# One core, two transformer blocks in float32: paired products counted once by the planner, a compression in quarters of the array, and 512-column tails and memory values

## The chip, the cores and the metric

The kernel runs on one core of one Trainium2 chip. The metric is the device time of one execution in microseconds (us); lower is better. The kernel before takes 2112.3 us, the median of three runs (2111.91 to 2114.06). The profiled execution took 2107.61 us, of which the span from the first to the last instruction is 2105.8 us.

## The reference

Two blocks, each of two layers, on 256 tokens of width 1024, all in float32.

- Block 1, per layer: `mixer1` (a gated linear recurrence, a forgetting attention with 8 heads that the kernel calls `fox`, a retention with 4 heads called `ret`), a cross attention to a memory of 256 rows (4 heads of 256), and a feed-forward part (`silu(h @ w_gate) * (h @ w_up)) @ w_down`, hidden width 2816).
- Block 2, per layer: a feed-forward part, `mixer2`, and a second feed-forward part. `mixer2` joins three attentions: a sparse one called `nsa` (8 heads), a stick-breaking one called `sb` (4 heads) and a window attention called `swa` (4 heads).

Of `nsa` one piece matters here, the compression of keys and of values:

```python
def compress(t, w1, w2):
    blocks = t[:, cmp_idx] + cmp_pos[:, None, :]        # 15 windows of 32 tokens, stride 16
    blocks = blocks.transpose(0, 3, 1, 2, 4).reshape(B, G, n_cmp, CMP_LEN * Dh)   # 2 * 15 rows of 2048
    return jax.nn.silu(blocks @ w1) @ w2                # w1: 2048 x 256, w2: 256 x 64
```

and of the cross attention the memory's keys and values, `mem_n @ w_k` and `mem_n @ w_v`, which depend on no earlier layer.

## The kernel before

**Weights.** Every weight passes through one class (`Weights`, from line 155). `plan` lists the chunks in the order of use. A chunk of at most 2048 columns (1 MB) is loaded by SP into one of three `raw` buffers. It is cut into pieces of 1024 columns, and each piece is split into a rounded part and a rest: ACT makes `whi` (the value cast to fp32r), DVE makes `wlo` (the raw value minus `whi`). Six pieces may be made ahead. A raw buffer comes free when its last piece is split, and then the next chunk is loaded. The activations are split in the same way (`thi`, `tlo`; `ahi`, `alo` in the feed-forward part; `mhi`, `mlo` for the memory), and a product is three matmuls: hi by hi, hi by lo, lo by hi (`mm3`). Small products of the attentions are plain float32; the profile shows each of those as two matmul records.

**Main and side work.** The products by the large weights are the main work, written in program order. Everything else (softmax, transposes, norms) is side work: Python generators in a list. After each half piece, `pump` (line 336) asks which generator's next step is due and writes it there. Due times come from `Pace` (line 49), a small model of the engines that is kept while the program is written: `nc.products` is when TensorE would be through with what is written so far, `nc.end` when a side step's results would be there. A step is written once its inputs are due by at most 0.3 us after `nc.products`. Where the main work needs a result that no step has delivered yet (`need`), `pump(force=True)` writes the remaining steps without main work between them. This document calls such a stretch forced.

**Pairs.** Two heads are worked on side by side: the first in the lower 64 rows or columns of the TensorE array, the second in the upper ones (`pair_scores`, `pair_scores_T`, `pair_pv`). `Pace` adds up the time of both.

**Feed-forward (`ffn`, planned at line 773).** The hidden width 2816 is five blocks of 512 columns and a tail of 256. For each block the gate products are made, ACT applies silu, the up products are made, DVE multiplies. The tail is two blocks of 256 columns, gate and up, each with its own accumulator of the two that rotate.

**Memory keys and values.** They are 16 units that fill gaps between other work (`fill_steps`, line 1170), each for 256 output columns: 48 matmuls of 256 columns, an ACT copy to `kvout` (one buffer) and a DMA to DRAM.

**Compression.** `compress_blocks` (line 1625) writes the windows, and `put` splits them on ACT and DVE. `compress_mm` (line 1647) then makes, for keys and values, 16 steps of `mm3` with 30 stationary and 256 moving columns: 96 matmuls in a layer, in eight pieces that stand between pieces of the gate weights. `compress_attention` (line 1727) transposes the result, and only there are the second weights `w2` and some small constants loaded, by SP, behind the large chunks in its queue. The output of `compress_attention` (`pcT`) is needed by the fourth and the eighth unit of `nsa`.

## Time and profile before

| what | value |
|---|---|
| median of three runs | 2112.3 us |
| profiled execution: its time, its span | 2107.61 us, 2105.8 us |
| mean granted TensorE clock | 0.995 of full speed |
| busy share: TensorE (PE), weight load, DVE, ACT, POOL | 97%, 82%, 61%, 53%, 4% |
| HBM read, mean rate | 372 MB, 180 GB/s |

Busy time of PE counts each matmul with its way through the array, so neighbours overlap. What a matmul adds to the time is the distance from its start to the next one's start, which the view in order of time shows. All lines read L150 because one helper records every instruction; groups are told apart by the names of the tiles.

### The profile page before, as it was taken

To read this page: it belongs to the slowest core of one execution; us is meant where nothing else is said; L and a number is where in the kernel's file an instruction comes from. 1 tells how busy PE (TensorE), PEld (TensorE's weight loads), DVE (VectorE), ACT (ScalarE), POOL (GpSimd) and SP (SyncE) were. 2 spreads that over 40 slices of the span, in tenths; PEclk is the share of its full clock that TensorE was granted. 3 is DMA by queue.
4 is the path that set the end of the run, shared out by engine and by line. 5 is a ranking of instruction groups with operands and counts; after the bars stand their busy time and mean duration, and the time that the engine had idled before them with its cause. 6 is when DMAs were issued, how large, how long until landed. Compare 5 with 4: busy or idle time off the path is not lost.

```text
span 2105.8 us, 28507 instructions
## 1 busy us (share of the span) xinstructions
PE 2053.1 (97%) x10982; PEld 1717.3 (82%) x10982; DVE 1276.0 (61%) x2187; ACT 1120.7 (53%) x1910; POOL 84.7 (4%) x110
## 2 busy tenths in 40 slices
PE   7999999999899999999999999999999999999999
PEld 6889888888797788788888767888888887768887
DVE  6766566556664755655467666664655567756553
ACT  5556566455465654555355655554555456446552
POOL 0210000002100000000001000000000001000000
PEclk9999999999999999999999999999999999999999
DMA  7555565654465565555646544555555547545553
GB/s 244 182 194 190 186 212 180 212 178 158 148 225 175 182 198 191 172 187 180 210 145 207 169 140 158 193 176 193 180 196 194 162 151 230 144 132 183 179 197 103
DMA packets 204583, 380.86 MB, mean 181 GB/s; under 512 B 14160, under 2 KB 78464, under 8 KB 204448
## 3 DMA queue, kind: packets, MB, share of 16 engines
q1 hardware_dynamic: 192928, 366.46, 53.1%
q10 hardware_dynamic: 11520, 12.59, 2.0%
q8 instruction: 86, 1.41, 0.3%
q14 instruction: 49, 0.40, 0.1%
HBM read 372.03 MB, written 6.99 MB: 180 GB/s over the span
## 4 chain that ended last, share of the span: by engine, by line
PE 83%; DVE 6%; ACT 4%; DMA 4%; issue 2%; POOL 0%; SPq 0%; ACTq 0%; DVEq 0%; POOLq 0%
PE acc L150 74%; PE aux L150 6%; DVE wlo L150 3%; PE o L150 3%; ACT whi L150 1%; DMA nb<-cdram 1%; DMA raw<-in_w_in_dram 1%; DMA w<-in_nsa_cmp_k_w_dram 1%; ACT rn L150 1%; ACT thi L150 1%; DMA kvd<-kvout 0%; SPq L150 0%; DVE t L150 0%; DVE h L150 0%; DMA mem<-in_mem_dram 0%
## 5 line engine op out<-in xcount | busy, mean ns | idle before, releaser
L150 PE MATMUL acc<-whi,thi 128*128 128x512 f32 (+2 forms) x1856 | 716.2, 386 | 2.3 <-ACT thi L150 1.4
L150 PE MATMUL acc<-whi,tlo 128*128 128x512 f32 (+2 forms) x1856 | 699.9, 377 | 2.5 <-DVE tlo L150 2.4
L150 PE MATMUL acc<-wlo,thi 128*128 128x512 f32 (+2 forms) x1856 | 699.3, 377 | 3.1 <-DVE wlo L150 2.8
L150 DVE TENSOR_TENSOR wlo<-raw,whi 128x1024 fp32r<-128x1024 f32 (+1 forms) x386 | 463.0, 1210 | 310.1 <-ACT whi L150 308.3
L150 ACT CAST whi<-raw 128x1024 fp32r<-128x1024 f32 (+1 forms) x386 | 393.7, 1037 | 243.9 <-PE acc L150 219.9
L150 DVE SCALAR_TENSOR_TENSOR wlo<-raw,prm,whi 128x512 fp32r<-128x512 f32 (+1 forms) x640 | 398.5, 680 | 173.8 <-ACT whi L150 173.6
L150 ACT ACTIVATE whi<-raw,prm 128x512 fp32r<-128x512 f32 (+1 forms) x640 | 379.9, 663 | 90.2 <-PE acc L150 86.7
L150 PEld LDWEIGHTS acc<-whi,thi 128*128 128x128 f32 x1856 | 350.3, 189 | 72.4 <-issue 9.3
L150 PEld LDWEIGHTS acc<-whi,tlo 128*128 128x128 f32 x1856 | 349.9, 189 | 70.3 <-DVE tlo L150 6.4
L150 PEld LDWEIGHTS acc<-wlo,thi 128*128 128x128 f32 x1856 | 350.5, 189 | 64.4 <-DVE wlo L150 6.1
L150 PE MATMUL acc<-whi,ahi 128*128 128x512 f32 x528 | 206.9, 392 | 0.0
L150 PE MATMUL acc<-whi,alo 128*128 128x512 f32 x528 | 205.7, 389 | 0.0
L150 PE MATMUL acc<-wlo,ahi 128*128 128x512 f32 x528 | 205.6, 389 | 0.0
L150 PEld LDWEIGHTS acc<-whi,alo 128*128 128x128 f32 x528 | 99.1, 188 | 20.8
L150 PEld LDWEIGHTS acc<-whi,ahi 128*128 128x128 f32 x528 | 99.2, 188 | 19.9
L150 PEld LDWEIGHTS acc<-wlo,ahi 128*128 128x128 f32 x528 | 99.2, 188 | 19.9
L150 POOL TENSOR_TENSOR r<-v,mhalf 128x1 f32<-128x1 f32 (+3 forms) x46 | 48.1, 1047 | 1593.9 <-DVE v L150 1591.9
L150 PE MATMUL acc<-thi,whi 128*128 128x256 f32 x384 | 111.9, 291 | 0.0
L150 PE MATMUL acc<-tlo,whi 128*128 128x256 f32 x384 | 108.6, 283 | 0.0
L150 PE MATMUL acc<-thi,wlo 128*128 128x256 f32 x384 | 108.5, 283 | 0.0
L150 DVE SCALAR_TENSOR_TENSOR silu<-acc,r,silu 128x512 f32<-128x512 f32 (+1 forms) x72 | 47.5, 702 | 100.4 <-PE acc L150 100.4
L150 ACT CAST ahi<-aux 128x512 fp32r<-128x512 f32 (+1 forms) x72 | 39.8, 553 | 121.9 <-PE aux L150 121.7
(301 smaller groups left out, 1946.9 us busy)
## 6 DMA issues: line engine op xcount, KB each, us to landing
raw<-in_w_in_dram SPq DMA_DIRECT2D x65, 1024.0 KB, 5.1
raw<-in_ffn_w_gate_dram SPq DMA_DIRECT2D x44, 1024.0 KB, 5.1
raw<-in_ffn_w_up_dram SPq DMA_DIRECT2D x44, 1024.0 KB, 5.1
raw<-in_ffn_w_down_dram SPq DMA_DIRECT2D x44, 1024.0 KB, 4.9
raw<-in_w_gate_dram SPq DMA_DIRECT2D x22, 1024.0 KB, 5.0
raw<-in_w_up_dram SPq DMA_DIRECT2D x22, 1024.0 KB, 5.1
raw<-in_w_down_dram SPq DMA_DIRECT2D x22, 1024.0 KB, 4.8
raw<-in_w_out_dram SPq DMA_DIRECT2D x16, 1024.0 KB, 5.0
```

What stands on the lines that cost most here:

```text
L150: return f(*args, **kwargs)
```

## The change

- `Pace` counts a product that runs beside another one at 7 ns in place of its columns. The second of each pair in `pair_scores`, `pair_scores_T` and `pair_pv` is marked so.
- Feed-forward tail: gate and up stand side by side in one 512-column block, loaded by two DMAs into one chunk. Silu and multiplication both follow the end of that block.
- Memory values: one accumulator for 512 columns, 48 matmuls of 512 for two units; one copy and one DMA for both. `kvout` is twice as large.
- Compression: `w1` is not split (`split=False`): the raw buffer itself is the moving operand, so it comes free only after the matmuls. The windows are not split either; they are padded to 32 columns with zeros. Four products at a time go to four column quarters of the array, in plain float32, and each quarter holds a part of the sum. A product by four stacked unit matrices (`sel`) adds the parts and transposes.
- The second weights and the constants are loaded when `compress_blocks` starts (`load_small`).
- `swa` waits for `blocks` where it waited for `blocks_ready`; `xs` in `mixer1` has one buffer in place of two.

```diff
-            self.products = start + max(0.027, size(moving) * rate / 2400.0) + 0.004
+            self.products = start + (0.007 if self.beside else max(0.027, size(moving) * rate / 2400.0) + 0.004)
...
-                mm(pss[u][:, c], q[HALF[u], qs], k[HALF[u], ks], start=True, stop=True)
+                mm(pss[u][:, c], q[HALF[u], qs], k[HALF[u], ks], True, True, beside=u > 0)
...
-            for w in (g, u):
-                W.plan(w, c0, c1, 0, 8, 4 if c1 - c0 == 512 else 8, 2 if c1 - c0 == 512 else 4, gain=gain)
+            if c1 - c0 == 512:
+                for w in (g, u):
+                    W.plan(w, c0, c1, 0, 8, 4, 2, gain=gain)
+            else:
+                W.plan(g, c0, c1, 0, 8, 4, 2, gain=gain, beside=u)
...
+                    if n < 512:
+                        hold["n"] = n
+                        gate_done(a)
...
-                    xs = mp.tile([P, 16, 32], F32, tag="xs", name=nm("xs"))
+                    xs = mp.tile([P, 16, 32], F32, tag="xs", name=nm("xs"), bufs=1)
...
+            W.plan(I["w_cv"][l], c // 2 * 512, c // 2 * 512 + 512, 4 * (c % 2), 4 * (c % 2) + 4, 4, 2)
...
+                            mm3(a[:, b * 512 : b * 512 + 512], MT.hi[:, kt, bs], MT.lo[:, kt, bs], hi[:, j, :], lo[:, j, :], kt == 0, kt == 7)
...
-                W.plan(I[f"nsa_cmp_{kv}_w1_2"][l], 0, 256, 8 * k, 8 * k + 8, 8, 4)
+                W.plan(I[f"nsa_cmp_{kv}_w1_2"][l], 0, 256, 8 * k, 8 * k + 8, 8, 4, split=False)
...
-                while "wqk_ready" not in hold or "blocks_ready" not in hold:
+                while "wqk_ready" not in hold or "blocks" not in hold:
...
-                            mm3(a[:30, k * S : k * S + S], bh[:, k, kt, :], bl[:, k, kt, :], hi[:, j, :], lo[:, j, :], kt == 0, kt == 15)
+                            mm(a[32 * j : 32 * j + 32, k * S : k * S + S], blocks[:, k, kt, :], w[:, j, :], i == 0, i == 3, beside=j > 0)
...
-                        turn(ps[:, (2 * k + b) * 30 : (2 * k + b + 1) * 30], raw[:, k * S + b * P : k * S + (b + 1) * P], ident[:30, :30])
+                        mm(ps[:, (2 * k + b) * 30 : (2 * k + b + 1) * 30], raw[:, k * S + b * P : k * S + (b + 1) * P], sel[:, :30], start=True, stop=True)
```

In numbers of matmuls: of the 256-column kind with `whi,thi` (and as many each with `wlo,thi` and `whi,tlo`) 224 become 32, while the 512-column kind goes from 1600 to 1696. For the memory values 128 of each of three kinds become 64 of 512 columns. The 192 compression matmuls become 64.

The first place is TensorE at the first piece of the compression in the first layer of `mixer2` (`o` is the accumulator of the compression, `t` the windows, `acc` the gate products ahead of it). Before, the last main product and the first 6 of 24 rows:

```order
L150 MATMUL acc_10173<-whi_10108,tlo_9112 128x512
L150 MATMUL o_10220<-whi_10126,t_796_10169 30x256
L150 MATMUL o_10220<-wlo_10127,t_796_10169 30x256
L150 MATMUL o_10220<-whi_10126,t_797_10170 30x256
L150 MATMUL o_10220<-whi_10126,t_796_10169 30x256
L150 MATMUL o_10220<-wlo_10127,t_796_10169 30x256
L150 MATMUL o_10220<-whi_10126,t_797_10170 30x256
```

Now, the whole of it:

```order
L151 MATMUL acc_9780<-wlo_9718,thi_8714 128x512
L151 MATMUL acc_9780<-whi_9717,tlo_8715 128x512
L151 MATMUL o_9818<-raw_9590,t_787_9645 32x256 x8
L151 MATMUL acc_9780<-whi_9771,thi_8714 128x512
L151 MATMUL acc_9780<-wlo_9772,thi_8714 128x512
```

Where 24 products stood, 8 stand, and they read the raw buffer.

The second place is TensorE at the end of the first layer of `mixer2`, where the main work needs all of `nsa` (`kT,qT` are a unit's scores, `ident,rn` its transposes, `rn,vsw` its products by the values, `bc,kk` the compressed part, `acc` the main work). Before, the last rows up to the forced stretch, and its first rows:

```order
L150 MATMUL aux_11302<-kT_9547,qT_9546 128x256
L150 MATMUL acc_11167<-whi_11121,thi_9111 128x512
...
L150 MATMUL acc_11333<-whi_11194,tlo_9542 128x512
L150 MATMUL o_11262<-rn_11287,vsw_9545 64x256
L150 MATMUL o_11262<-rn_11289,vsw_9545 64x256
L150 MATMUL o_11262<-rn_11287,vsw_9545 64x128
L150 MATMUL o_11262<-rn_11289,vsw_9545 64x128
L150 MATMUL aux_11357<-ident_90,rn_11309 128x128 x3
L150 MATMUL aux_11358<-ident_90,rn_11314 128x128 x3
```

Now, at the same scores:

```order
L151 MATMUL acc_10772<-whi_10652,tlo_9145 128x512
L151 MATMUL aux_10790<-kT_9150,qT_9149 128x128
L151 MATMUL aux_10791<-kT_9150,qT_9149 128x128
L151 MATMUL aux_10790<-kT_9150,qT_9149 128x256
L151 MATMUL aux_10791<-kT_9150,qT_9149 128x256
L151 MATMUL o_10814<-rn_10766,vsw_9148 64x256
L151 MATMUL o_10814<-rn_10768,vsw_9148 64x256
L151 MATMUL o_10814<-rn_10766,vsw_9148 64x128
L151 MATMUL o_10814<-rn_10768,vsw_9148 64x128
L151 MATMUL aux_10819<-ident_90,rn_10798 128x128 x3
L151 MATMUL aux_10820<-ident_90,rn_10803 128x128 x3
```

The forced stretch began at the values of the sixth unit; now it begins at those of the fifth, and four units' products by the values stand in it where three stood.

The third place is SP's queue around the compression weights of the first layer of `mixer2` (`w20` and `w21` are the second weights; the semaphores in brackets are the engines or queues waited for). Before:

```order
L150 DMA raw182_10195<-in_nsa_cmp_v_w1_2_dram 128x8x256 [waits DMAHW7_49,DVE_49]
L150 DMA raw183_10237<-in_w_in_2_dram 128x4x512 [waits DMAHW0_49,DVE_49]
L150 DMA raw184_10277<-in_nsa_cmp_v_w1_2_dram 128x8x256 [waits DMAHW1_49,DVE_49]
L150 DMA raw185_10315<-in_w_in_2_dram 128x4x512 [waits DMAHW2_49,DVE_49]
...
L150 DMA raw190_10609<-in_w_up_swa_2_dram 64x2x1024 [waits DMAHW5_49,DVE_49]
L150 DMA raw190_10609<-in_w_up_swa_2_dram 64x2x1024
L150 DMA w20_856_10666<-in_nsa_cmp_k_w2_2_dram 128x2x64 [waits DMAHW6_49]
L150 DMA w21_857_10667<-in_nsa_cmp_v_w2_2_dram 128x2x64 [waits DMAHW7_49]
```

Now:

```order
L151 DMA raw178_9590<-in_nsa_cmp_k_w1_2_dram 128x8x256 [waits DMAHW5_49,DMAHW0_49,DVE_49]
L151 DMA w20_781_9633<-in_nsa_cmp_k_w2_2_dram 128x2x64
L151 DMA w21_782_9634<-in_nsa_cmp_v_w2_2_dram 128x2x64
...
L151 DMA raw182_9833<-in_nsa_cmp_v_w1_2_dram 128x8x256 [waits DMAHW2_49,PE_49]
L151 DMA raw183_9855<-in_w_in_2_dram 128x4x512 [waits DMAHW3_49,DMAHW1_49,DVE_49]
L151 DMA raw184_9899<-in_nsa_cmp_v_w1_2_dram 128x8x256 [waits DMAHW4_49,DMAHW0_49,PE_49]
L151 DMA raw185_9955<-in_w_in_2_dram 128x4x512 [waits DMAHW3_49,DMAHW2_49,PE_49]
```

The small weights moved ahead of twelve large chunks, and chunks 182, 184 and 185 wait for TensorE where they waited for DVE.

## Rows read from the trace of the kernel before

**Rows 1.** The page, busy time and share of the span of TensorE.

```profile
PE 2053.1 (97%) x10982; PEld 1717.3 (82%) x10982; DVE 1276.0 (61%) x2187; ACT 1120.7 (53%) x1910; POOL 84.7 (4%) x110
```

**Rows 2.** The page, the chain that ended last, share of the span by engine.

```profile
PE 83%; DVE 6%; ACT 4%; DMA 4%; issue 2%; POOL 0%; SPq 0%; ACTq 0%; DVEq 0%; POOLq 0%
```

**Rows 3.** In order of time: start, duration, matmul, in a feed-forward part and its tail.

```profile
1399.64 0.39 PE L150 MATMUL acc<-whi,thi 128*128 128x512 f32 x1
...
1405.08 0.39 PE L150 MATMUL acc<-whi,thi 128*128 128x512 f32 x1
...
1419.08 0.28 PE L150 MATMUL acc<-whi,thi 128*128 128x256 f32 x1
...
1421.96 0.28 PE L150 MATMUL acc<-whi,thi 128*128 128x256 f32 x1
```

**Rows 4.** Groups by form: count, busy time, mean ns, idle before.

```profile
L150 PE MATMUL acc<-whi,thi 128*128 128x256 f32 x224 | 64.5, 288 | 0.0
L150 PE MATMUL acc<-mhi,whi 128*128 128x256 f32 x128 | 37.9, 296 | 0.0
L150 PE MATMUL o<-whi,t 128*30 128x256 f32 x128 | 24.1, 280 | 1.3 <-DVE t L150 1.3
```

**Rows 5.** In order of time, 24 compression matmuls, first and last.

```profile
1164.32 0.28 PE L150 MATMUL o<-whi,t 128*30 128x256 f32 x1
...
1166.99 0.28 PE L150 MATMUL o<-whi,t 128*30 128x256 f32 x1
```

**Rows 6.** In order of time, a pair of heads by the values, eight records.

```profile
1209.40 0.39 PE L150 MATMUL acc<-whi,tlo 128*128 128x512 f32 x1
1209.72 0.87 PE L150 MATMUL o<-rn,vsw 128*64 128x256 f32 x8
1210.52 0.50 PE L150 MATMUL acc<-whi,thi 128*128 128x512 f32 x1
1210.87 0.40 PE L150 MATMUL acc<-wlo,thi 128*128 128x512 f32 x1
```

**Rows 7.** Chain in order of time: start, duration; four plain float32 products, cross attention.

```profile
200.09 1.73 PE o L150 x8
```

**Rows 8.** Waits of TensorE in the whole run: total us, times, longest.

```profile
PE aux L150 <- DMA w<-in_nsa_cmp_k_w_dram: 3.8, 2, 2.6
PE aux L150 <- DVE rs L150: 2.9, 2, 1.5
...
PE o L150 <- DVE rvg L150: 2.2, 1, 2.2
...
PE acc L150 <- ACT kvout L150: 1.9, 1, 1.9
PE aux L150 <- DVE rot L150: 1.7, 2, 1.5
```

**Rows 9.** In order of time, the forced stretch in `mixer2`, first layer.

```profile
1253.94 0.87 PE L150 MATMUL o<-rn,vsw 128*64 128x256 f32 x8
...
1261.35 1.44 PE L150 MATMUL aux<-ident,rn 128*128 128x128 f32 x6 [2.06 <-DVE rn L150]
1262.73 2.24 PE L150 MATMUL o<-rn,vsw 128*64 128x256 f32 x8
1264.89 1.27 PE L150 MATMUL o<-bc,kk 128*128 128x256 f32 x4
1266.84 0.50 PE L150 MATMUL acc<-whi,thi 128*128 128x512 f32 x1 [0.68 <-ACT thi L150]
```

**Rows 10.** Groups by form: silu of a tail, split of a piece.

```profile
L150 DVE TENSOR_TENSOR wlo<-raw,whi 128x1024 fp32r<-128x1024 f32 x376 | 457.0, 1226 | 307.7 <-ACT whi L150 306.0
L150 ACT CAST whi<-raw 128x1024 fp32r<-128x1024 f32 x376 | 388.6, 1049 | 243.9 <-PE acc L150 219.9 <-DVE rot L150 9.4 <-DMA raw<-in_w_in_dram 6.9
...
L150 ACT ACTIVATE silu<-acc,r 128x256 f32<-128x256 f32 x12 | 5.0, 471 | 13.7 <-PE acc L150 13.7
```

**Rows 11.** The page, DMA issues: KB each, median us from issue to landing.

```profile
raw<-in_nsa_cmp_k_w_dram SPq DMA_DIRECT2D x4, 1024.0 KB, 5.2
```

More of the change, by code (lines that the diff above doesn't have):

```diff
@@ L61, in __init__ @@
         self.loads = 0.0
+        self.beside = False
         for name in ("tensor", "vector", "scalar", "gpsimd", "sync"):
@@ L164, in __init__, with plan @@
         self.limit = None
-    def plan(self, ap, c0, c1, k0, k1, a_chunk, a_piece, split=True, gain=None, halves=0):
+    def plan(self, ap, c0, c1, k0, k1, a_chunk, a_piece, split=True, gain=None, halves=0, beside=None):
         b = c1 - c0
@@ L177, in plan @@
                 parts = [(slice(0, P), ap[k * P : (k + a) * P, c0:c1].rearrange("(a p) n -> p a n", p=P))]
-            self.chunks.append((parts, a, b))
+            parts = [(ps, slice(0, b), v_) for ps, v_ in parts]
+            if beside is not None:
+                parts.append((slice(0, P), slice(b, 2 * b), beside[k * P : (k + a) * P, c0:c1].rearrange("(a p) n -> p a n", p=P)))
+            self.chunks.append((parts, a, b * (1 if beside is None else 2)))
             for j in range(0, a, a_piece):
                 n = min(a_piece, a - j)
-                self.pieces.append([ci, j, n, b, split, j + n >= a, None, list(range(k + j, k + j + n)), gain])
+                self.pieces.append([ci, j, n, b * (1 if beside is None else 2), split, j + n >= a, None, list(range(k + j, k + j + n)), gain])
     def start(self, n):
@@ L320, in tile_two_blocks, with mm @@
     sides = []
-    def mm(ps, a, b, start, stop):
+    def mm(ps, a, b, start, stop, beside=False):
+        nc.beside = beside
         nc.tensor.matmul(ps, a, b, start=start, stop=stop)
+        nc.beside = False
     def turn(ps, src, by):
@@ L416, in pair_scores_T @@
             for u in (0, 1):
-                mm(pss[u][:, c], k[HALF[u], ks], q[HALF[u], qs], start=True, stop=True)
+                mm(pss[u][:, c], k[HALF[u], ks], q[HALF[u], qs], True, True, beside=u > 0)
         return pss
@@ L441, in pair_pv @@
             for u in (0, 1):
-                mm(dst[HALF[u], q0:S], vs[u][:, kt, :], ws[u][:, c0:c1], start=start and kt == 0, stop=stop and kt == 1)
+                mm(dst[HALF[u], q0:S], vs[u][:, kt, :], ws[u][:, c0:c1], start and kt == 0, stop and kt == 1, beside=u > 0)
     def put_T(T, kt0, ob):
@@ L1174, in fill_steps @@
         for l, kind, c in todo:
-            a = acc()
+            if kind == "k" or c % 2 == 0:
+                a = acc()
             for i in (0, 1):
@@ L1190, in fill_steps @@
                             mm(ps, lo[:, j, bs], MT.hi[:, kt, :], start=False, stop=last and b == 1)
-                        else:
-                            mm3(a[:, b * 512 : b * 512 + S], MT.hi[:, kt, bs], MT.lo[:, kt, bs], hi[:, j, :], lo[:, j, :], first, last)
                 W.done(idx)
-                if i == 1:
-                    o = mem["pool"].tile([P, 2, S], F32, tag="kvout", name=nm("kvout"), bufs=1)
-                    nc.scalar.copy(o, a[:, :512].rearrange("p (b n) -> p b n", b=2) if kind == "k" else a.rearrange("p (b n) -> p b n", b=2)[:, :, :S])
+                if i == 1 and kind == "k":
+                    o = mem["pool"].tile([P, 2, 2, S], F32, tag="kvout", name=nm("kvout"), bufs=1)[:, 0]
+                    nc.scalar.copy(o, a[:, :512].rearrange("p (b n) -> p b n", b=2))
                     nc.sync.dma_start(kvd[l, kind][c], o.rearrange("p b n -> p (b n)"))
+                elif i == 1 and c % 2 == 1:
+                    o = mem["pool"].tile([P, 2, 2, S], F32, tag="kvout", name=nm("kvout"), bufs=1)
+                    nc.scalar.copy(o, a.rearrange("p (b c n) -> p c b n", b=2, c=2))
+                    nc.sync.dma_start(kvd[l, kind][c - 1 : c + 1].rearrange("c p n -> p c n"), o.rearrange("p c b n -> p c (b n)"))
                 pump()
@@ L1303, in rotary_tables @@
         for dst, shift in ((sin, 0.0), (cos, 0.25)):
-            w = mem["pool"].tile([P, 2, S], F32, tag="kvout", name=nm("ang"), bufs=1)
+            w = mem["pool"].tile([P, 2, 2, S], F32, tag="kvout", name=nm("ang"), bufs=1)[:, 0]
             a, n = w[:, 0, :64], w[:, 1, :64]
@@ L1623, in nwin_done, with load_small @@
                 side(nsa())
+            def load_small():
+                w2 = [one([P, 2, 64], f"w2{k}") for k in (0, 1)]
+                for k, n in ((0, "k"), (1, "v")):
+                    nc.sync.dma_start(w2[k], I[f"nsa_cmp_{n}_w2_2"][l].rearrange("(b p) d -> p b d", p=P))
+                kbd, vmask, valid = const(mp, "kbd"), const(mp, "vbd"), const(mp, "cvalid")
+                bc = one([P, S], "bc")[:, :240]
+                nc.sync.dma_start(bc, bcmp)
+                hold["small"] = w2, kbd, vmask, valid, bc
             def compress_blocks():
+                load_small()
                 d = hold["dup"]
-                blocks = hold["blocks"] = t4()[:, :960].rearrange("p (k j m) -> p k j m", k=2, j=16)
+                blocks = t4().rearrange("p (k j m) -> p k j m", k=2, j=16)
+                nc.gpsimd.memset(blocks[:, :, :, 30:], 0.0)
                 yield True
@@ L1727, in compress_attention @@
             def compress_attention(a):
-                raw = t2()[:30]
-                nc.scalar.copy(raw, a[:30])
+                raw = t2()
+                nc.scalar.copy(raw, a)
+                sel = one([P, 32], "sel")
+                nc.vector.tensor_reduce(sel, ident.rearrange("p (j m) -> p m j", j=4), axis=AX.X, op=ALU.add)
                 hold["cmp"] = True
@@ L1741, in compress_attention @@
                 yield True
-                w2 = [one([P, 2, 64], f"w2{k}") for k in (0, 1)]
-                for k, n in ((0, "k"), (1, "v")):
-                    nc.sync.dma_start(w2[k], I[f"nsa_cmp_{n}_w2_2"][l].rearrange("(b p) d -> p b d", p=P))
-                kbd, vmask, valid = const(mp, "kbd"), const(mp, "vbd"), const(mp, "cvalid")
-                bc = one([P, S], "bc")[:, :240]
-                nc.sync.dma_start(bc, bcmp)
+                w2, kbd, vmask, valid, bc = hold["small"]
                 hk, tk = hid[:, 0], th_[:, 0]
```

31 lines of the change are left out of this document (17 added, 14 removed).

## The prediction

> **What bounds the kernel now.** I read the page first. TensorE is busy for 97% of the span and the next engine, DVE, for 61% [rows 1], and the chain that ended last runs over TensorE for 83% of it [rows 2]. So time is lost or won where TensorE's own work changes, or where TensorE waits. Busy time won't do as a price, because neighbouring matmuls overlap; the price is the distance between starts, from the view in order of time [rows 3]. From 1399.64 to 1405.08 lie 24 matmuls of 512 columns, so one costs 5.44/24 = 0.2267 us. From 1419.08 to 1421.96 lie 24 of 256 columns, 0.120 each. Two of 256 cost 0.240 where one of 512 costs 0.2267: 13.3 ns are paid per matmul beside its columns. The waits of TensorE came next [rows 8]. They are short and few, most of them in the mixers, where side steps stand between main products. Last I read the stretch at the end of `mixer2`, where main work stops until `nsa` is through [rows 9]: TensorE has gaps there that no main work fills.
>
> **Tails, gain 3.8 us.** Of the 256-column kind 224 - 32 = 192 products go for each of three operand pairs [rows 4], 576 in all, and 288 of 512 come. 576 x 0.120 = 69.1, 288 x 0.2267 = 65.3. The feed-forward part is bound by TensorE alone there (no gap in rows 3), so all of it counts. ACT and DVE get fewer and longer splits, which nobody waits for. The cost: silu now follows the whole block. Two silu of 0.47 each [rows 10] and two multiplications of like length stand between the last product and the reuse of that accumulator. The first token tile's silu can run while the second tile is multiplied, and the down products start on the other accumulator with six matmuls (6 x 0.2267 = 1.36). What isn't covered lies between 0 and 0.9 us a part (one split ahead in ACT's queue, 1.05 [rows 10], less what is left of the cover); I take 0.1 for each of six, 0.6.
>
> **Memory values, gain 2.6 us.** 3 x 128 matmuls of 256 [rows 4] become 192 of 512: 46.1 - 43.5.
>
> The Trainium skill's page "TensorE: Matmul & The Clock Gate" (section "Back-to-back issue gap") gives N/2.4 GHz plus about 2.5 ns for a single matmul. By that both merges together would give an estimated 480 x 2.5 ns = 1.2 us instead of 6.4. Here the measured 13.3 ns decides.
>
> **Compression, gain 12.3 us.** Before, 23 starts take 2.67 us [rows 5], 0.116 each; in two layers 192 of them, 22.3. Now there are 64 products in 16 groups of four. No row shows four quarters at once, so I bound it. A pair of 64 columns each, two products of 256 and two of 128 columns, takes 0.80 from its start to the next main product [rows 6]; the first main product behind it takes 0.35 where 0.227 is usual, and the one ahead 0.32: 0.2 for changing over. Four plain float32 products of 256 that don't run together take 1.73 [rows 7], 0.43 each. If the four quarters run together, a group costs about 0.45, a step of two groups about 1.0, and with 0.2 for the change 1.2; eight such steps and 0.4 for the two that are cut in half make 10.0. If only two run together the 16 groups cost 16 x 0.86 + 2 = 15.8, and if none do, 16 x 1.73 + 2 = 29.7, 7.4 more than before. On the other side it can't be under 16 x 0.43 = 6.9. I take 10.0, since pairs run fully together in rows 6. The splits that go (16 pieces and the windows) lay on ACT and DVE; one wait of TensorE of 1.3 us in all, for the split windows, goes with them (the idle before, in [rows 4]).
>
> **Small weights first, gain 3.8 us.** TensorE waited twice for them [rows 8]. They are now asked for at `nkv_done`, before all of the compression; SP spends some six short issues on them ahead of one large chunk, whose products are many microseconds away. What is late next in that chain is the arithmetic of `compress_attention` itself, which steps behind main products.
>
> **The planner's pairs.** With the second of a pair nearly free, `nc.products` runs slower against ACT and DVE, so side steps are written behind more main products. Three kinds of waits of steps written too early should go: for `rs` 2.9 (24 more main products now stand ahead of those transposes), and in the second `mixer1` for `rvg` 2.2, `rot` 1.7 and `kvout` 1.9 [rows 8]; together 8.7. The price is paid at the ends, where the same steps remain to be done without cover:
> - In `mixer2` one more unit of `nsa` falls into the forced stretch. The unit there before it waited 2.06 for its scaled scores [rows 9]; two layers, 4.1.
> - `swa`'s last step now stands right before the main work that needs it. A forced end looks like this [rows 9]: the products by the values take 2.16 (1262.73 to 1264.89) where 0.80 is usual [rows 6], 1.4 lost on the copies; the last four take 1.95 where 0.87 is due (half of [rows 7]), 1.1 lost on the split. 2.5 in all, of which a unit's transposes cover some 0.5: 2.0 a layer, 4.0.
> - `fox` in both `mixer1` likewise ends right before the main products that need it: 2 x 2.5 = 5.0.
>
> **Edits I cost at nothing.** One `xs` buffer: DVE waits for POOL, while it is idle 39% of the time and pieces are made ahead; between 0 and some 2 us a layer. The wider `kvout`, the `sel` reduction, two memsets: off the path. A raw buffer that is held until TensorE is through: chunk 185 is asked for at the end of the third compression step. It needs 5.2 to land [rows 11] and 1.05 and 1.23 for the split [rows 10], 7.5. Ahead of its first use stand 24 main products (5.4), a pair of scores (0.9) and a compression step (1.2), 7.5. It just fits; the bounds are 0 and the third rival.
>
> **Sum.** 3.8 + 2.6 + 12.3 + 1.3 + 3.8 + 8.7 = 32.5 gained, 0.6 + 4.1 + 4.0 + 5.0 = 13.7 paid, net 18.8 less. The profiled execution's 2107.6 would become 2088.8. The median of the runs stands 4.7 above that execution, so the forecast is 2112.3 - 18.8 = 2093.5, rounded 2093.
>
> **Rivals.**
> 1. *The quarters don't run together.* For it: no trace here shows four, and all four quarters share the rows of the array and one bank. Against it: the pairs in rows 6 share both too. Two at a time, 5.8 of the gain goes: 2099. One at a time, 19.7 goes: 2113. The same page of the Trainium skill ("Packing small matmuls — row/col tiling") says that a weight load overlaps running products only when the row group differs, which the quarters don't do; that would put the groups between these cases. Its table has 2.38 times for three column tiles, an estimated 64 x 0.43/2.38 = 11.6 us. The pairs in rows 6, in one row group too, show no such loss.
> 2. *The side chains already set the ends of the mixers.* Then what TensorE saves there comes back as forced waiting. For it: rows 9, and the order of the changed program, where one more unit is forced. Against it: in the first layer the forced stretch takes 12.9 us, 1253.94 to 1266.84 [rows 9], and main products stand right before it. If the mixers gave nothing, only the tails and the memory values remain, 6.4 - 0.6: 2106. If forced ends cost twice my price besides, 2112.
> 3. *Slower: raw buffers held by the compression starve the main products.* Four chunks in a layer (182, 184, 185, 187) wait for TensorE, and SP issues in order, so chunks behind them wait too. If a chunk also finds the one before it still landing, 5.2 more is exposed. Eight chunks times 5.2 is 41.6, less 18.8: 2135. It decides from 18.8/8 = 2.4 us exposed per chunk. Against it: the first three such chunks have two main chunks and more ahead of their use.
>
> **How the numbers follow.** The forecast case has 0.69, with its own range 2081 to 2103: below, forced ends at half price (6.5), quarters at their floor (3.1) and some short waits that rows 8 leave out (3); above, `xs` uncovered (4), silu uncovered (4.8). Rival 1 has 0.11 (two thirds of it two at a time), rival 2 0.12, rival 3 0.08. 0.2% of this kernel, 4.2 us, is about what a measurement can tell from no change. Faster: 0.69, 0.07 of rival 1 (two at a time) and 0.07 of rival 2 (at 2106), together 0.83; within 0.2%: 0.04 and 0.05, the rest of these two, 0.09; slower: 0.08, rival 3. The range 2073 to 2108 leaves out the top of rivals 1 and 2 and all of 3, and reaches below the case's own range, since waits that vanish could be more than the listed ones.
>
> **What would show it.** Right: compression steps of eight products with some 1.0 us between their first start and the next main product; no wait for `w` in front of `hh`; starts 0.227 apart through the tails; TensorE's wait for `rvg` and `rot` gone and a wait at `thi` or `rn` before the main products in both mixers; `mixer2` some 6 us shorter a layer. Wrong: groups of 1.7 us (rival 1); a forced stretch in `mixer2` of over 20 us (rival 2); waits of `acc` for `whi` or of `o` for `raw` in the compression (rival 3).

## The result

The changed kernel takes 2146.1 us (median of 4 runs, 2144.0 to 2147.6), beside it the kernel before 2112.1 (2105.5 to 2114.1): 1.0166 times, 95% interval 1.0142 to 1.0190, 34 us slower. I had forecast 2093, range 2073 to 2108, and gave slower a chance of 0.08. The prediction was wrong in its sign.

On the page after, TensorE has a longer span with less in it: its share of the span fell from 97% [rows 1] to 96%, and in the chain TensorE keeps 83% and "issue" rises from 2% [rows 2] to 3%.

```profile
PE 2067.2 (96%) x10446; PEld 1692.5 (79%) x10446; DVE 1250.7 (58%) x2123; ACT 1096.1 (51%) x1840; POOL 90.2 (4%) x112
...
PE 83%; DVE 6%; ACT 4%; DMA 4%; issue 3%; POOL 1%; SPq 0%; ACTq 0%; DVEq 0%; POOLq 0%
```

TensorE's waits in the whole run after (total, times, longest) show that only some of what I had said would go did go. The waits for the small weights `w` and for `rvg` [rows 8] are gone. `rs` is down from 2.9 to 1.8 at the transposes, but has a new 1.6 at `o`; `rot` and `kvout` grew. Beside them stand longer ones:

```profile
PE aux L151 <- DVE rn L151: 9.3, 6, 2.3
PE acc L151 <- ACT kvout L151: 6.5, 2, 4.2
PE aux L151 <- DVE ta L151: 6.0, 2, 3.0
PE aux L151 <- DVE kcb L151: 5.8, 2, 2.9
...
PE aux L151 <- DVE cpr L151: 3.8, 2, 3.0
PE aux L151 <- DMA hk<-ud: 3.7, 1, 3.7
...
PE aux L151 <- DVE rot L151: 2.8, 1, 2.8
```

Two views narrow it down. The first is ACT's list of waits in the whole run: how long ACT stood before a split because the raw chunk of a main product had not landed. The first line is the kernel before, the second after.

```profile
ACT whi L150 <- DMA raw<-in_w_in_dram: 6.9, 5, 2.8
```

```profile
ACT whi L151 <- DMA raw<-in_w_in_dram: 37.9, 13, 5.9
```

The second is the end of `mixer2` in the first layer, in order of time (start, duration, matmul, and in brackets the idle time and what ended it). Before, the stretch without main products ran for 12.9 us [rows 9].

```profile
1273.18 0.93 PE L151 MATMUL aux<-kT,qT 64*128 64x128 f32 x8
1274.03 0.87 PE L151 MATMUL o<-rn,vsw 128*64 128x256 f32 x8
1277.18 1.16 PE L151 MATMUL aux<-ident,rn 128*128 128x128 f32 x6 [2.27 <-DVE rn L151]
1278.45 2.01 PE L151 MATMUL aux<-kT,qT 64*128 64x128 f32 x8
1280.38 1.55 PE L151 MATMUL o<-rn,vsw 128*64 128x256 f32 x8
1283.11 1.59 PE L151 MATMUL aux<-ident,rn 128*128 128x128 f32 x6 [1.18 <-DVE rn L151]
1284.63 2.34 PE L151 MATMUL aux<-kT,qT 64*128 64x128 f32 x8
1286.90 1.55 PE L151 MATMUL o<-rn,vsw 128*64 128x256 f32 x8
1289.63 1.59 PE L151 MATMUL aux<-ident,rn 128*128 128x128 f32 x6 [1.18 <-DVE rn L151]
...
1294.90 0.50 PE L151 MATMUL acc<-whi,thi 128*128 128x512 f32 x1 [0.68 <-ACT thi L151]
```

The main products end ahead of the scores at 1273.18, and the next one comes at 1294.90: 21.7 us. Behind these first scores (`kT,qT`) those of two more units stand in the stretch, where the stretch before had one; products by the values (`rn,vsw`) stand there four times (the last at 1291.15 is left out above), where they stood three times; and three times the transposes wait for scaled scores. The windows on these two stretches (columns: length, then busy time of PE, PEld, DVE, ACT and POOL, granted clock, DMA share, GB/s) show a second price. The first line is the kernel before, the second after:

```profile
1253.94:1266.84 12.90, 9.05 (x49) 5.32 (x48) 5.01 (x22) 4.41 (x14) 0.00 (x0) 0.87 0.00 1
```

```profile
1273.20:1294.90 21.70, 16.25 (x79) 9.73 (x78) 7.66 (x43) 9.10 (x32) 0.00 (x0) 0.69 0.04 13
```

TensorE is busy for 16.25 of the 21.70 us, and the granted clock is 0.69 of 2.4 GHz, so part of the stretch ran at 1.2. By the profile's records the clock fell at 1279.2, behind the wait of 2.27, and rose at 1292.8. The scores at 1273.18 and the values at 1274.03 take 0.93 and 0.87; between the fall and the rise they take 2.34 (1284.63) and 1.55 (1286.90).

### The profile page after: what moved, and what is told of

Its sections match the earlier page's. It is cut to its first block, busy times and chain, and to the rows that moved or that the text cites. A ratio compares the mean times of both kernels' runs of the same rounds, so it can differ in the third digit from the quotient of the medians.

```text
span 2145.8 us, 27307 instructions
## 1 busy us (share of the span) xinstructions
PE 2067.2 (96%) x10446; PEld 1692.5 (79%) x10446; DVE 1250.7 (58%) x2123; ACT 1096.1 (51%) x1840; POOL 90.2 (4%) x112
## 4 chain that ended last, share of the span: by engine, by line
PE 83%; DVE 6%; ACT 4%; DMA 4%; issue 3%; POOL 1%; SPq 0%; ACTq 0%; DVEq 0%; POOLq 0%
PE acc L151 73%; PE aux L151 7%; DMA raw<-in_w_in_dram 2%; DVE wlo L151 2%; PE o L151 2%; ACT whi L151 1%; ACT rn L151 1%; ACT thi L151 1%; DVE h L151 0%; DMA mem<-in_mem_dram 0%; ACT cpr L151 0%; DMA nb<-cdram 0%; DVE ngm L151 0%; DVE tlo L151 0%; DMA bt<-btiles 0%
## 5 line engine op out<-in xcount | busy, mean ns | idle before, releaser
L151 PE MATMUL acc<-whi,thi 128*128 128x512 f32 (+1 forms) x1760 | 701.5, 399 | 10.8 <-ACT kvout L151 6.5
L151 PE MATMUL acc<-wlo,thi 128*128 128x512 f32 (+1 forms) x1760 | 685.1, 389 | 5.0 <-DVE wlo L151 4.7
L151 PE MATMUL acc<-whi,tlo 128*128 128x512 f32 (+1 forms) x1760 | 685.2, 389 | 2.5 <-DVE tlo L151 2.4
L151 DVE TENSOR_TENSOR wlo<-raw,whi 128x1024 fp32r<-128x1024 f32 (+1 forms) x370 | 442.3, 1208 | 302.1 <-ACT whi L151 300.4
L151 ACT CAST whi<-raw 128x1024 fp32r<-128x1024 f32 (+1 forms) x370 | 378.3, 1036 | 274.1 <-PE acc L151 221.7
L151 DVE SCALAR_TENSOR_TENSOR wlo<-raw,prm,whi 128x512 fp32r<-128x512 f32 (+1 forms) x592 | 392.3, 717 | 178.2 <-ACT whi L151 178.0
L151 ACT ACTIVATE whi<-raw,prm 128x512 fp32r<-128x512 f32 (+1 forms) x592 | 371.6, 694 | 93.3 <-PE acc L151 89.8
L151 PEld LDWEIGHTS acc<-whi,thi 128*128 128x128 f32 x1760 | 333.4, 189 | 88.1 <-issue 11.2
L151 PEld LDWEIGHTS acc<-whi,tlo 128*128 128x128 f32 x1760 | 332.6, 189 | 75.1 <-DVE tlo L151 7.1
L151 PEld LDWEIGHTS acc<-wlo,thi 128*128 128x128 f32 x1760 | 333.5, 189 | 71.4 <-DVE wlo L151 9.1
L151 ACT ACTIVATE silu<-acc,r 128x512 f32<-128x512 f32 (+1 forms) x72 | 43.1, 650 | 127.7 <-PE acc L151 127.6
```

The costliest lines, as they stand in the source:

```text
L151: return f(*args, **kwargs)
```

## The experiments

All times are compared with the kernel before on the same chip, and differences between kernels are taken from these ratios. "Old estimate" means the planner as it was before. The last six columns are from each profile: from the first matmul, or the last down product of the part before, to the first scores of `cross` (mixer1); from there to the last side matmul in the gate and up products (cross); from the last down product to that same point (mixer2 of both layers); and the stretch without main products at the end of `mixer2`, both layers.

| kernel | us | ratio, 95% interval | mixer1 | cross | mixer2 | stretch |
|---|---|---|---|---|---|---|
| before | 2109 | 1 | 184.7, 178.4 | 180.5, 181.0 | 355.5, 357.2 | 12.9, 11.8 |
| after | 2146.1 | 1.0166 (1.0142-1.0190) | 192.0, 179.4 | 183.1, 186.0 | 366.7, 369.0 | 21.7, 23.0 |
| e1 old estimate | 2133.3 | 1.0115 (1.0094-1.0137) | 184.6, 178.6 | 184.6, 186.1 | 366.1, 368.1 | 9.8, 8.4 |
| e2 new estimate alone | 2121.6 | 1.0061 (1.0043-1.0080) | 188.9, 180.2 | 180.5, 180.7 | 361.3, 357.5 | 22.6, 21.2 |
| e3 tails and values | 2119.4 | 1.0047 (1.0026-1.0067) | 185.3, 178.8 | 184.6, 185.9 | 356.7, 357.1 | 11.8, 12.9 |
| e4 compression | 2125.8 | 1.0083 (1.0062-1.0104) | 183.9, 176.9 | 180.5, 180.7 | 366.9, 364.1 | 8.4, 8.4 |
| e5 ... copied | 2097.6 | 0.9945 (0.9925-0.9964) | 184.1, 178.2 | 180.5, 181.1 | 351.3, 350.0 | 6.2, 6.2 |
| e6 tails | 2111.3 | 1.0009 (0.9994-1.0025) | 186.7, 180.7 | 180.4, 181.4 | 355.5, 359.5 | 12.6, 13.8 |
| e7 values, one `xs` | 2113.6 | 1.0023 (1.0008-1.0037) | 185.5, 176.1 | 184.6, 183.3 | 355.7, 357.1 | 12.6, 12.6 |
| e8 null | 2100.5 | 0.9962 (0.9946-0.9979) | 185.4, 170.1 | 180.5, 180.7 | 355.4, 354.6 | 13.6, 11.8 |
| e9 after, copied | 2133.6 | 1.0119 (1.0102-1.0136) | 189.7, 177.0 | 184.8, 185.8 | 359.4, 363.3 | 22.7, 22.9 |
| e10 values, bias 10 | 2109.9 | 1.0011 (1.0000-1.0022) | 184.4, 176.4 | 180.5, 181.4 | 357.0, 360.1 | 11.8, 13.9 |
| e11 e5 + null | 2090.8 | 0.9919 (0.9900-0.9937) | 186.1, 173.4 | 180.5, 180.6 | 351.4, 350.9 | 6.2, 6.2 |
| e12 e2 + null | 2117.8 | 1.0044 (1.0030-1.0058) | 186.1, 179.6 | 180.5, 181.8 | 359.2, 358.5 | 23.3, 21.9 |
| e13 work, mended | 2097.5 | 0.9943 (0.9925-0.9961) | 184.3, 179.8 | 180.4, 180.3 | 350.3, 350.2 | 6.2, 6.2 |
| e14 pair at a quarter | 2124.4 | 1.0070 (1.0052-1.0088) | 184.4, 179.5 | 180.5, 180.8 | 364.9, 363.4 | 22.8, 21.8 |
| e15 e13 + null | 2087.9 | 0.9906 (0.9891-0.9921) | 187.1, 168.6 | 180.4, 181.1 | 350.9, 350.9 | 6.2, 6.2 |
| e16 e13 + 13.3 ns | 2101.2 | 0.9962 (0.9950-0.9973) | 194.9, 170.4 | 182.9, 180.2 | 350.1, 350.1 | 2.6, 2.6 |

What is left of the span, the feed-forward parts between these stages, differs by at most 0.3 us a part in all of them.

### First four: the parts alone

My first theory was that the new estimate alone lost it all. e1 takes only the estimate back out of the changed kernel (for the pairs, and for the quarters of the compression, which are marked in the same way); e2 to e4 add one part each to the kernel before.

```
e1:  -   self.products = start + (0.007 if self.beside else max(...) + 0.004)
     +   self.products = start + max(0.027, size(moving) * rate / 2400.0) + 0.004
e2:  before + beside=u > 0 in the pairs' products and the 0.007 in Pace
e3:  before + FFN tails of 512 + memory values of 512 + xs bufs=1
e4:  before + compression in quarters (split=False) + load_small()
```

> The changed kernel, but the estimate counts the second product of a pair at its full length again; all edits of work stay. Theory 1 (the estimate writes side steps too late, and that alone made the kernel slower): the gains of the work come through, 2112 - 23 (tails 3.2, memory values 2.6, compression and its split 13.6, small weights 3.8) = about 2089; the forced stretches at the ends of the mixers are no longer than before. Theory 2 (compression that holds raw buffers is what costs): 2130 to 2140. Theory 3 (the 512-column memory values make TensorE wait for kvout): 2100 to 2105, with a wait for kvout of over 4 us left in the first mixer1.

> The kernel before with the new estimate for pairs alone. Theory 1: slower by the whole difference, 2112 + 34 + 23 = about 2169, with waits for rn, rot and cpr as in the changed kernel. Theories 2 and 3: what I forecast for this part, 2112 - 8.7 + 13.1 = 2117.

> The kernel before with the 512-column tails and memory values (and one xs buffer, for space) alone, old estimate. My terms: 2112 - 3.2 - 2.6 = 2106. Theory 3: no gain or some loss, 2112 to 2116, through waits for kvout.

> The kernel before with the compression in quarters and the small weights loaded first alone, old estimate (two xs buffers). My terms: 2112 - 12.3 - 1.3 - 3.8 = 2095. Theory 2: slower, 2130 to 2140, with waits of acc for whi or of o for raw. If quarters did not run together: about 2112.

Theory 1 fell. e1 is still 24 us slower than before, so the estimate costs 11 of the 35 (1.0166 of 2109), and e2 alone costs 13. Theory 3 fell too: the wait for `kvout` in e3 is 1.8, no longer than before [rows 8]. Theory 2 gave 2130 to 2140 for both e1 and e4; e1 lies in that range and e4 below it. Every part by itself makes the kernel slower: 13, 10 and 17.5 us, in sum 40. The table says where: the estimate in `mixer1` and `mixer2`, the tails and values in `cross`, the compression in `mixer2`.

### Held raw buffers: e5

How a raw buffer that is held reaches TensorE can be read in the changed kernel's own trace, in one place of `mixer2`: SP, then ACT, then DVE, then TensorE.

```profile
1137.48 0.38 SPq L151 DMA_DIRECT2D raw<-in_w_in_dram  x1
1144.51 0.38 SPq L151 DMA_DIRECT2D raw<-in_nsa_cmp_k_w_dram  x1
1153.39 0.37 SPq L151 DMA_DIRECT2D raw<-in_w_in_dram  x1
...
1158.49 1.99 ACT L151 CAST whi<-raw 128x1024 fp32r<-128x1024 f32 x2 [5.85 <-DMA raw<-in_w_in_dram]
...
1159.57 2.36 DVE L151 TENSOR_TENSOR wlo<-raw,whi 128x1024 fp32r<-128x1024 f32 x2 [4.25 <-ACT whi L151]
1161.84 0.95 DVE L151 TENSOR_TENSOR ta<-wqk,r 128x768 f32<-128x768 f32 x1
...
1162.85 0.71 PE L151 MATMUL aux<-ident,ta 128*128 128x128 f32 x3 [2.99 <-DVE ta L151]
```

There are three raw buffers. The compression keeps two of them, so all main chunks pass through the third, one at a time. SP can't ask for the next until the one before is split, at 1153.39, 15.9 us after the last main chunk; ACT stands 5.85 us before the split of that chunk; DVE stands 4.25 behind ACT, with its part of the same split at the head of its queue; and `ta`, which needs no weight at all, sits behind that split. TensorE waits 2.99 for it. Such a wait carries the name of a side step, and only the two lists of the engines in front show that a load is its cause. e5 keeps the quarters and gives the raw buffer back early:

```
+            if split == "copy":
+                hi = self.pool.tile([P, PIECE], F32R, tag="hi", ...)
+                w = hi[:, : a * b].bitcast(F32)
+                nc.scalar.copy(w, raw.rearrange("p a n -> p (a n)"))
+                ...            (then releases the raw buffer, as a split does)
-  W.plan(I[f"nsa_cmp_{kv}_w1_2"][l], ..., 8, 4, split=False)
+  W.plan(I[f"nsa_cmp_{kv}_w1_2"][l], ..., 8, 4, split="copy")
```

> The kernel before with quarters and small weights first, as in e4, but ACT copies each compression piece out of its raw buffer in plain float32, so that the buffer goes back to SP when the copy is done and not when TensorE is through. Theory A (held raw buffers are what costs in e4, 2126): the gain that I forecast for these parts shows, 2095 to 2100; the load that feeds the main products is asked for as early as before and the waits for ta, rn and merged in mixer2 shrink from 35 us in all to under 10. Theory B (the shorter compression gives the side chains less cover, so that they end late whatever the buffers do): 2115 to 2126 as in e4.

2097.6: 28 us better than e4, with 16 more copies on ACT. `mixer2` falls from 366.9 and 364.1 to 351.3 and 350.0. A new draw of the order, which the section on e8 prices at 8 us, doesn't explain it: in all five kernels with copies and the old estimate (e5, e11, e13, e15, e16) a layer of `mixer2` takes 350.0 to 351.4 us, in the two with held buffers and the old estimate (e1, e4) 364.1 to 368.1. TensorE's waits for `ta`, `rn` and `merged`, which the expectation named, fall from 34.4 to 5.6 in the whole run. In e4, and then in e5, where none for `ta` is left:

```profile
PE aux L151 <- DVE rn L151: 19.2, 6, 4.2
...
PE aux L151 <- DVE ta L151: 8.9, 2, 5.2
PE acc L151 <- DVE merged L151: 6.3, 2, 3.3
```

```profile
PE aux L151 <- DVE rn L151: 5.1, 4, 1.7
...
PE acc L151 <- DVE merged L151: 0.5, 2, 0.2
```

ACT's wait, in e4 and then in e5:

```profile
ACT whi L151 <- DMA raw<-in_w_in_dram: 27.6, 9, 7.3
```

```profile
ACT whi L151 <- DMA raw<-in_w_in_dram: 7.6, 5, 3.3
```

That is theory A, the third rival of the prediction. In the same run the stretch at the end falls to 6.2 us though the compression is shorter, so theory B does not hold here.

### A step that falls one place later: e6, e7, e10

> The kernel before with the 512-column tails alone. My term: 2109 - 3.2 = 2106. Theory C (every edit that shifts the planner's clock moves a side step past the main products that covered it): slower by some 4 to 8, with a forced step in cross. By e3's trace the tails give back in the down products what they gain: 2109 apart from such a step.

> The kernel before with the 512-column memory values and one xs buffer alone. My term: 2109 - 2.6 = 2106.5. Theory C: slower, 2113 to 2120, and cross longer by 4 to 5 a layer as in e3.

The tails alone are within 0.2% of before (1.0009) and `cross` is not longer, so theory C does not hold for them. The values alone are 5 us slower, all of it in `cross` (6.4 more there, 1.5 less in `mixer1`), where none of their products lie. The order there shows why. `c,rb` is the bias chain for `mixer2`; it is due 12 us of estimated time after `cross` begins, and `finish(bias)` at the end of `cross` stops the main products until the chain is through. In e7:

```profile
208.22 0.63 PE L150 MATMUL aux<-ident,cpr 128*128 128x128 f32 x4
...
210.20 0.81 PE L150 MATMUL aux<-c,rb 32*12 32x383 f32 x2
...
225.14 1.99 PE L150 MATMUL aux<-mk,cqT 128*128 128x256 f32 x8 [1.17 <-ACT cqT L150]
230.14 1.09 PE L150 MATMUL aux<-ident,cpr 128*128 128x128 f32 x4 [3.01 <-DVE cpr L150]
```

The bias step stands behind the transposes, and at the end twelve main products that used to lie between the last scores and the transposes of `cpr` stand behind `finish`, so TensorE waits 3.01 for `cpr`. e10 is e7 with two numbers changed:

```
-        yield nc.products + 12.0            (bias_rows; 12.0 in bias_squares too)
+        yield nc.products + 10.0
```

> The 512-column memory values and one xs buffer (as e7, 2114), with the bias chain of cross due 10 us after its layer's cross begins, not 12. Theory C: in e7 the estimated clock of cross had shifted so that the first bias step came one place later, behind the transposes, and finish(bias) then stopped the main products; with 10 it takes its old place, cross takes 180.5 and 181 us again instead of 184.6 and 183.3, and the time is about 2107, what I forecast for the edit. If what costs is a wait for the memory's stores or the one xs buffer: 2114 as e7.

`cross` is back at 180.5 and 181.4, and in the trace of e10 the bias step stands ahead of the transposes again, without a wait for `cpr`:

```profile
206.40 0.81 PE L150 MATMUL aux<-c,rb 32*12 32x383 f32 x2
207.14 0.66 PE L150 MATMUL aux<-ident,cpr 128*128 128x128 f32 x4
```

So neither the stores nor the single `xs` buffer cost anything that shows in `cross`. The whole came to 2109.9 and not 2107: `mixer2` is 1.5 and 2.9 longer.

### How far the draw of places goes: e8, e11, e16

```
e8:  -   self.products = start + max(0.027, size(moving) * rate / 2400.0) + 0.004
     +   self.products = start + max(0.027, size(moving) * rate / 2400.0) + 0.006
```

> The kernel before, with one number of the estimate changed from 4 to 6 ns per product; no work changes. Theory C (the order is tuned, and any shift of the planner's clock costs some): slower by 4 to 12. Theory D (small shifts don't matter, what costs is each edit's own doing): within 2 us of 2109.

8 us faster, with no work changed; 8.3 of it in the second `mixer1`, where the waits for `rvg` and `kvout` [rows 8] went. Theory C had the size and the wrong direction, theory D is out: a shift of 2 ns per product in the planner's clock moves this kernel by more than most of the edits I was pricing. So a difference of less than some 8 us between two of these kernels can be put down to an edit only where a trace shows the place. e11 puts it on e5, and e16 moves the mended kernel (e13, below) by more:

> e5 (quarters copied, small weights first) with 6 ns per product in the estimate as in e8. e8 gained 8.3 us in the second mixer1 alone, which e5 doesn't touch: if the two add, 2097.6 - 8.5 = 2089. If orders don't add (a shift of the clock draws new places everywhere): anywhere from 2085 to 2110.

> e13 with 13.3 ns per product in the estimate, which is what the trace shows. It makes the planner's products slower against the other engines, so that steps are written earlier in count of products. If the loss of the new estimate was lost slack, more of it should help or be even: 2088 to 2097. If any shift draws new places: up to 2110.

In e11 (2090.8) the shift gave 5.5 us of the 8, and not in one place: the second `mixer1` is 4.8 shorter than in e5, the first 2.0 longer. e16 counts each product with the measured 13.3 ns, and its stretch at the end falls to 2.6 us, as more slack should have it; but its first `mixer1` takes 194.9 where e13 has 184.3, its second 170.4 where e13 has 179.8, and in all it is 4 us slower than e13, outside the 2088 to 2097 expected. So more slack shortened the stretch at the end, and in `mixer1` it went both ways; which size suits which stage stays open.

### The estimate for pairs: e9, e12, e14

> The changed kernel with all its parts, and the compression pieces copied out of the raw buffers as in e5. If the held buffers are a cost of their own that adds to the other parts: 2146 less the 28 between e4 and e5, 2118. If the new estimate alone makes the side chains late whatever the buffers do: no better than 2130.

> The new estimate for pairs alone (e2, 2121.6) with 6 ns per product that is counted. Theory P (paired products that count as nearly nothing put steps late, and the forced stretches that this adds stay): the forced stretch of mixer2 stays at 20 us or more, 2115 to 2125. Theory C alone (only the draw of places): the time moves by 8 us or more either way, and the forced stretch may come back to 13 us.

> The kernel before with the second of a pair counted at a quarter of its length, so that a pair in the estimate takes 0.80 us, as the trace shows it (before 1.30, changed 0.66). Theory Q (the new number is too small, and only that puts steps late): 2105 to 2111, forced stretch of mixer2 of 13 to 15 us. Theory P (the old number, too large, was slack that the side chains need; a true one is as harmful): 2115 to 2122, forced stretch of 19 us or more.

e14 differs from e2 by one factor:

```
-  self.products = start + (0.007 if self.beside else max(...) + 0.004)
+  self.products = start + ((0.25 if self.beside else 1.0) * max(...) + 0.004)
```

In every kernel with a new estimate, e2, e9, e12 and e14, the stretch at the end of `mixer2` is 21 to 23 us; in every one with the old it is 13.9 or less. Shifting the clock (e12) doesn't take it away, mending the buffers (e9) doesn't, and neither does counting a pair as what the trace shows [rows 6] (e14, 14.8 us slower than before, 2 above the range of theory P). So theory Q fell and theory P stands: the old number, 1.30 us for a pair that takes 0.80, was slack. It made the planner's TensorE slow, so steps of the side chains were written early in count of main products, and enough main products were left to cover the last units. e9 came to 2133.6, not 2118: with the estimate in it, mending the buffers gives back 10 us and not 28. TensorE's waits for `ta` and `kcb` go, 11.8 in all, but those for `tlo` (at `acc`) and `wng` grow from 3.7 to 10.7, and the stretch at the end of `mixer2` stays at 23 us. The two costs overlap.

### The work alone, mended: e13, e15

e13 has all edits of work, the old estimate, the copied pieces and the bias chain due at 10; e15 is e13 with 6 ns.

> All edits of work together under the old estimate, with the two mishaps mended: compression pieces copied out of the raw buffers, bias chain due 2 us earlier. My terms for these edits: 2109 - 23 = 2086. From the parts as they measured: e5 2097.6, and +1.9 for the memory values (e10), +2.4 for the tails (e6): 2102. If the mishaps were only part of what e1 lost: 2115 or more.

> e13 (all edits of work, both mishaps mended, old estimate) with 6 ns per product in the estimate. If the gain of e8 in the second mixer1 adds: 2097.5 - 7 = 2090, with mixer1 of the second layer at 170 to 174 us instead of 179.8. If places are drawn anew without an order in it: 2088 to 2105.

2097.5 and 2087.9. e15 beats both kernels: 0.9906 of before (0.9891 to 0.9921), 20 us. The two mishaps and the estimate, which the changed kernel has and e13 has not, make 47 us between them.

## Why the prediction was wrong, by its steps

**The raw buffer that is held, costed at nothing ("It just fits").** This failed, and it is the largest single error: 28 us between e4 and e5, 10 within the full change (after to e9). I had followed one chunk, 185, and added up what stands ahead of its first use in TensorE's order, 7.5 against 7.5. Two mistakes are in that sum. It had no room for a second held buffer, with which the main chunk in front is asked for late too. And it asked who needs the chunk on TensorE; the price was paid earlier, on ACT and DVE, where the split of a late chunk stands in order ahead of side steps that need no chunk. Rival 3 named the mechanism and the place to look ("waits of `acc` for `whi` or of `o` for `raw`"), but the sign I gave was wrong as well: those waits stayed short, 1.4 us for `whi` in the whole run, and the time shows under `ta` and `kcb` instead (in e4 under `ta`, `rn` and `merged`).

**The granted clock, not in the sum at all.** I priced a wait by its length. But behind many waits the clock falls to 1.2 GHz, as in the stretch above, and the products there take longer. Of the profiled spans 23 us ran at the lower level before, 58 in e2 and 87 after (mean granted clock 0.995, 0.987 and 0.980). An estimate, from each distance between starts at the lower level less the median distance of the same two matmuls at the upper one: this costs 10 us before, 24 in e2 and 36 after. TensorE's listed waits add up to 47, 49 and 72. So e2's loss of 13 us is nearly all clock, 14 against 2 of longer waits; and of the 40 us by which the profiled execution after is longer, waits make 25 and the clock 26, with some 11 of saved work against them. The same oversight is in my reading of [rows 9]. I took the 2.16 from 1262.73 for 0.80 and 1.4 lost on copies; it ran at a granted clock of 0.50. In the second layer before, at a clock of 1.00, the same products take 1.30:

```profile
1262.73:1264.89 2.16, 2.16 (x9) 1.20 (x8) 0.00 (x0) 0.48 (x1) 0.00 (x0) 0.50 0.00 0
```

```profile
1878.29 1.38 PE L150 MATMUL o<-rn,vsw 128*64 128x256 f32 x8
1879.59 1.13 PE L150 MATMUL o<-bc,kk 128*128 128x256 f32 x4
```

**The planner's pairs, 8.7 gained and 13.1 paid.** The gain failed: of the four waits that I said would go, only the one for `rvg` went. `rs` has 3.4 in all where it had 2.9, `rot` 2.8 where it had 1.7, `kvout` 6.5 where it had 1.9: 12.7 in place of 8.7. In ACT's order of time in the first `mixer1` the copy that TensorE waits for stands behind scores that wait for DVE, and behind two splits:

```profile
146.44 0.40 ACT L151 ACTIVATE sc<-sc,ngm 128x128 f32<-128x128 f32 x1 [1.08 <-DVE ngm L151]
...
147.50 1.97 ACT L151 CAST whi<-raw 128x1024 fp32r<-128x1024 f32 x2
149.38 1.00 ACT L151 COPY kvout<-acc 128x1024 f32<-128x1024 f32 x1
```

For the forced ends I had 4.1 for one more unit in both layers and 4.0 for `swa`, together 4.05 a layer; the stretch grew by 8.8 and 11.3 us. Not all of that is lost: it holds one more unit, as I had read from the order (6.2 us, 1278.45 to 1284.63), whose matmuls stood between main products before. What the stages lost is in the table. In e2, with the estimate alone, `mixer2` is 6.1 longer in both layers together, where my terms there were 8.1 paid and 2.9 gained, 5.2 net; `mixer1` is 6.0 longer, where they were 5.0 paid and 5.8 gained. So in e2 the step that failed is the gain in `mixer1`. Within the full change (e1 to after) 8.2 lie in `mixer1` and 1.5 in `mixer2`; where the buffers are given back (e13 to e9, which differ in the bias chain too) it is 2.6 and 22.2. The net of the estimate's part, which I put at 13.1 - 8.7 = 4.4 lost, measured 11 (after to e1) and 13 (e2). Rival 2 gave "over 20 us" as its sign, and that came; its price, 2112 at most, was too low.

**Not in the sum either: steps that fall elsewhere in stages that the change doesn't touch.** `cross` lost 2.6 and 5.0 us through a bias step that was one place later. I read the order where the change puts instructions, in the mixers, and not where its shorter products shift the clock.

**Compression, 10.0 us for 16 groups.** The mechanism and the size were right. After, eight products that share the array run in one step, 1.00 us from first start to the next main product, as predicted:

```profile
1152.19 0.39 PE L151 MATMUL acc<-whi,tlo 128*128 128x512 f32 x1
1152.51 1.07 PE L151 MATMUL o<-raw,t 128*32 128x256 f32 x16
1153.51 0.50 PE L151 MATMUL acc<-whi,thi 128*128 128x512 f32 x1
```

Rival 1 is out. The Trainium skill, page "TensorE: Matmul & The Clock Gate", section "Packing small matmuls — row/col tiling", lets a weight load overlap running products only in another row group. Here the trace differs: all quarters use all rows, their records show weight loads of 0.11 beside running products of 0.38, and a step has no more loss than the change-over of a pair. The 17.4 that I put on compression, its wait and the small weights came out as 11.6 in e5, once the buffers are free. A draw of the order is in that number too. Of the rest, 3 us show as a longer wait for `rs` (5.9 in that run, 2.9 before [rows 8]); what became of the other 3 stays open.

**Small weights.** No wait for `w` is left after, as predicted. With the old estimate the edit decides it: kernels without it wait 3.2 to 4.1 (before, e3, e6, e7, e8, e10), kernels with it not at all. With the new estimate the order does so as well: e2 and e12, without the edit, have no such wait, and e14 has 8.9.

**Tails, 3.8 less 0.6.** The pitch of 0.2267 [rows 3] holds through the tails, but the silu cost was mis-sized. Before, and then after:

```profile
383.48 0.39 PE L150 MATMUL acc<-whi,alo 128*128 128x512 f32 x1
383.71 0.38 PE L150 MATMUL aux<-ident,silu 128*128 128x128 f32 x2
383.85 0.48 PE L150 MATMUL acc<-whi,ahi 128*128 128x512 f32 x1
```

```profile
393.41 0.39 PE L151 MATMUL acc<-whi,alo 128*128 128x512 f32 x1
393.89 0.44 PE L151 MATMUL aux<-ident,silu 128*128 128x128 f32 x2
394.37 0.47 PE L151 MATMUL acc<-whi,ahi 128*128 128x512 f32 x1
```

From the sixth down product to the next lie 0.96 us; in the kernel before the same place took 0.37. The 0.59 more, six times, is 3.5 where I had 0.6: the whole gain, inside the bounds of 0 to 0.9 that I had given, and I took the wrong end. e6 shows no gain: the rest of a feed-forward part, with the tail in it, takes 69.0 us in its trace and 68.9 before.

**Memory values, 2.6.** The line that I named for them in [rows 4], `mhi,whi`, is that of the keys, which stay at 128 products of 256 columns; the values are `whi,mhi`, as many before and 64 of 512 after, so the sum stands. Not shown to gain: e10 is at 1.0011. The edit's own products lie in `mixer1`, which is 2.3 shorter there in both layers together, about the forecast, but a draw of places of that size can't be told from it.

**The `xs` buffer, costed at nothing.** It can't be told apart from the values; `mixer1` in e10, 0.3 and 2.0 shorter than before, shows no sign of the 2 us a layer that I gave as the bound.

Taken together, about half of the work's terms came: without the estimate, 23 gained were forecast and e13 gained 12. e15's 20 hold the shift of the clock as well, which is a lucky draw and says nothing of the terms. The rest was the belief that these gains reach the end of the run by themselves. Three things that I took as given, early release of buffers, a tuned order, and slack in the estimate, were worth more than all of the products saved.

## What to carry to other kernels

A buffer that now waits for a slower reader must be priced on every engine that stands in order behind the loads it delays, not at the one product that uses it. Where a planner sets the order, a truer cost is not a better one; change it by itself, look at the ends where its slack was used, and time a null shift of its numbers before pricing an edit of a few microseconds. A wait shows the name of the last step in a chain: follow it back one engine at a time before believing it. And look at the granted clock behind a wait: its price can be more than its length.

## What the runs showed that I had not expected

- A change of 2 ns per product in the planner's clock, without any change of work, moved the time by 8 us (e8).
- Eight plain float32 products of 256 columns on quarters of the array take 1.00 us from their first start to the next main product, where four on the whole array take 1.73 [rows 7].
- In the longer stretch without main products at the end of `mixer2` the granted clock was 0.69 in the first layer and 0.63 in the second, where it had been 0.87 and 1.00 in the shorter ones, so waits there cost more than their length.
